# Cross attention's output projection as seven products, with its right operands stored during the first FFN

## The chip, the cores and the metric

The kernel runs on one core of a Trainium2 chip, as one launch. The metric is the device time in microseconds (us), the median of the runs shown. Profiles show one execution, whose span goes from the first to the last instruction.

## The reference

One decoder layer on 1024 tokens of width 1024, in float32, with 256 memory tokens:

```
x <- LN1(alpha*x + 1/2 * SwiGLU_1(x))          D_FF = 2816
x <- LN2(alpha*x + W_out[HGRN2(x) ; SGU(x)])   token mixers
x <- LN3(alpha*x + CrossAttn(x, LN_m(mem)))    4 heads of 256
x <- LN4(alpha*x + 1/2 * SwiGLU_2(x))

def _memory_cross_attention(h, mem, mem_g, mem_b, wq, wk, wv, wo):
    m = _layer_norm(mem, mem_g, mem_b)
    q = (h @ wq).reshape(B, T, X_HEADS, X_HEAD_DIM)
    ...
    p = jax.nn.softmax(s, axis=-1)
    o = jnp.einsum('bhtm,bmhd->bthd', p, v).reshape(B, T, D_MODEL)
    return o @ wo
```

The change concerns the last line, `o @ wo`, a product of 1024 x 1024 by 1024 x 1024, and the sum and norm LN3 behind it.

## The kernel before

Matrix products keep float32 precision by splitting each operand into a high and a low part of type float32r (`split`, `split_w`: ACT copies the high part, DVE subtracts it for the low one). Each product is three matmuls in one bank of PSUM (`mm3`): high by high, high by low, low by high. A matmul takes 128 rows of the contraction and writes 128x512.

The activations stand transposed in SBUF, in two halves of 512 tokens: `xh[half]` and `xl[half]`, eight k-tiles of 128 features each. Weights are read by `load_split`: a load of 512 KB on SP's queue into one of three raw buffers, then the split.

The stages follow each other on TensorE: the start (the memory's norm on GpSimd and ACT, its transposes `ptm`, its keys `psk` and values `psv`, and x transposed, `pt_x`), FFN 1 (up projections `st_gf` and `st_uf` in Strassen's form, then the down projection `dp_f`), the token mixers, their output projection `acc_mx`, cross attention, its output projection `acc_xa`, and FFN 2. FFN 2's first pair of feature tiles (`pg_f`, `pu_f`) is multiplied without Strassen's form, one half of the tokens after the other, so that it can begin while the other half is still normed.

The order of instructions on each engine comes from a scheduler that plays the program through in time. Work that follows a product on other engines is written as a coroutine: `spawn` starts it, it yields the time (in us) of other products that should come first, and `tick(us)` moves all of them on. Waits are taken by each engine in its fixed order.

The output projection runs in three groups of token tiles, (0,1), (2,3,4) and (5,6,7), by `down_group`: for each of eight k-tiles it loads and splits a 128x1024 piece of `xa_w_o`, so it reads the weight three times (`wd_xa`, 24 loads), and multiplies with both column halves. The first group is woven into the attention of the second half of the tokens. Behind a group, `residual_norm` adds the residual on DVE, norms each tile, stores it to `res[2]` and transposes it (`pt_xa`) into `xh` and `xl`, with a copy `xf_xa` for FFN 2's combinations.

Cross attention makes queries `paq`, scores `pss`, probabilities transposed `ptp`, and in `attend` the outputs `pao`, which are split straight from PSUM into `xh` and `xl`.

Before, no DMA is issued by GpSimd; all data transfers go through SP's queue.

Of the kernel before, what the change touches and what calls it, by code (L numbers as in the profile page):

```python
# [15 lines left out]
P = 128  # L16
# [8 lines left out]
H = 4  # L25
# [3 lines left out]
WARM = 32  # L29
LEVELS = [64, 32, 16, 8, 4, 2, 1]  # L30
# [3 lines left out]
def hybrid_layer_kernel(ctx: ExitStack, tc: tile.TileContext, a, out):  # L34
# [29 lines left out]
    # Work that follows a matrix product on other engines runs as a coroutine: where the tensor  # L64
    # engine would wait for it, it yields the time of other products (in us) to issue first.
# [26 lines left out]
    # the tensor engine's clock rises while it works: transposes until the first tile is there  # L92
# [9 lines left out]
    # left and right operands of the products of the FFNs' down projection, by pair of feature tiles  # L102
    lops = dram.tile([7, NF // 2, P, HALF], F32, name="lops")
    rops = dram.tile([2, NF // 2, P, HALF], F32, name="rops")
    res = [dram.tile([T, D], F32, name=f"res{i}") for i in range(3)]

# [5 lines left out]
    def load_raw(view, name, pool=None):  # L112
        if pool is not None:
            raw = pool(f"{name}_r", [P] + list(view.shape[1:]))
            nc.sync.dma_start(raw, view)
            return raw
        raw = wpool.tile([P] + list(view.shape[1:]), F32, tag="raw", bufs=3, name=f"{name}_r")
        nc.sync.dma_start(raw, view)
        return raw
# [10 lines left out]
    def mm3(ps, lh, ll, rh, rl, first, last):  # L130
        nc.tensor.matmul(ps, lh, rh, start=first, stop=False)  # L131
        nc.tensor.matmul(ps, lh, rl, start=False, stop=False)  # L132
        nc.tensor.matmul(ps, ll, rh, start=False, stop=last)  # L133
# [73 lines left out]
    def layer_norm(y, gb, bb, name):  # L207
        """y: [P, 1024] tile, normalized over its free dim in place."""
# [5 lines left out]
    def residual_norm(tt, lag, acc, res_src, gb, bb, dst, name, keep=None):  # L214
        """dst = LN(alpha * res_src + acc) for a token tile, and its transpose."""
# [10 lines left out]
    def down_group(w, nk, grp, operand, res_src, gb, bb, dst, name, keep=None):  # L226
        """dst = LN(alpha * res_src + operand^T @ w) for the token tiles of grp; yields after each k."""
# [20 lines left out]

    def half_sl(hf):
# [28 lines left out]
    def w_combos(w, f1, f2, name, pool=None):  # L278
        """Left operands of the products, in two stages: those of the first part, then all."""
# [48 lines left out]
    def ffn(wg, wu, wd, g, b, res_src, dst, make_xT, xf, name, start=None):  # L328
        """start: products that come before, given what to do late in them; without it, the first pair of
        feature tiles is multiplied without Strassen's form."""  # L330
# [17 lines left out]
        else:  # L348
            f0 = 2
            wts, hts = {}, {}  # L350
            for f, hf in ((0, 0), (1, 0), (0, 1), (1, 1)):
                if (f, hf) == (0, 1):
# [5 lines left out]
                if (f, hf) == (1, 1):  # L358
                    wc[1] = combos(1, f0)
                    ready_u = next(wc[1])  # L360
                if hf == 0:
# [845 lines left out]
```

## Time and profile before

| | |
|---|---|
| time, median of 3 runs | 2039.55 us (2039.29 to 2039.57) |
| span of the profiled execution | 2032.8 us |
| what lies around the span, median less span | 6.75 us |
| TensorE busy | 2015.5 us (99%) |
| DVE, ACT, GpSimd busy | 1504.1, 890.0, 102.5 us |
| first and last product of `acc_mx` | about 1022 and 1152 us |
| output projection `acc_xa` | about 1275 to 1386 us |

How to read it: PE is TensorE's matmul, PEld its weight load, DVE is VectorE, ACT ScalarE, POOL GpSimd, SP the engine that issues DMAs. L131 is line 131 of the kernel, and a line may be that of a helper. A row of a group gives the busy time, the mean length of one in ns, the idle time of the engine just before them and what ended it. Matmuls are pipelined, so the length of one is more than its distance to the next.

### The profile page before, as it was taken

The page shows a single profiled execution, that of the slowest core. Times are in us where ns is not written, and L with a number is a line of the kernel's source. Part 1 is how long each engine was busy: PE and PEld are TensorE (multiplying, and loading weights), DVE is VectorE, ACT ScalarE, POOL GpSimd, SP SyncE. Part 2 cuts the span into 40 slices and gives each one's busy share as a digit, 9 for nine tenths or more (in the row PEclk, how much of TensorE's full clock was granted, in tenths as well). Part 3 has the DMA queues.
Part 4 walks back from the last instruction along what each step waited for, and adds up shares of the span by engine and source line. Part 5 has one row for each costly group of instructions (what it writes and reads, how often), then busy time and mean ns, then how long its engine had stood idle before and what let it go on. Part 6 is the DMA issues. An engine that isn't in the chain of part 4 may idle for free.

```text
span 2032.8 us, 25339 instructions
## 1 busy us (share of the span) xinstructions
PE 2015.5 (99%) x9646; PEld 1689.1 (83%) x9646; DVE 1504.1 (74%) x2246; ACT 890.0 (44%) x1239; POOL 102.5 (5%) x144
## 2 busy tenths in 40 slices
PE   8999999999999999999999999999999999999998
PEld 7888888888888888888888888888888888888886
DVE  5987677677668967948796855678776776776688
ACT  6633333334533467547644344444333333344432
POOL 0000000000002010100110100010000000000021
PEclk8999999999999999999999999999999999999999
DMA  8333233237887632123156522353232332378874
GB/s 263 122 114 119 78 114 119 78 119 250 290 289 261 222 116 73 53 63 105 41 176 228 162 88 74 122 197 119 88 126 82 104 127 81 109 249 291 297 254 172
DMA packets 244250, 306.88 MB, mean 151 GB/s; under 512 B 14368, under 2 KB 154272, under 8 KB 244128
## 3 DMA queue, kind: packets, MB, share of 16 engines
q1 hardware_dynamic: 244128, 305.26, 45.3%
q8 instruction: 76, 1.25, 0.2%
q14 instruction: 46, 0.38, 0.1%
HBM read 234.44 MB, written 70.78 MB: 150 GB/s over the span
## 4 chain that ended last, share of the span: by engine, by line
PE 93%; DVE 3%; DMA 2%; POOL 1%; issue 1%; SPq 0%; ACT 0%; POOLq 0%; DVEq 0%; ACTq 0%
PE st_gf L131 7%; PE st_uf L131 7%; PE st_gf L133 7%; PE st_uf L133 7%; PE st_gf L132 7%; PE st_uf L132 7%; PE dp_f L133 6%; PE dp_f L131 6%; PE dp_f L132 6%; PE psl L939 2%; PE acc_xa L131 1%; PE acc_xa L133 1%; PE acc_xa L132 1%; PE paq L131 1%; PE paq L133 1%; PE paq L132 1%
## 5 line engine op out<-in xcount | busy, mean ns | idle before, releaser
L132 PE MATMUL dp_f<-wd_f_l,ah_f 128*128 128x512 f32 x552 | 213.3, 390 | 0.0
L131 PE MATMUL dp_f<-wd_f_h,ah_f 128*128 128x512 f32 x552 | 208.4, 390 | 0.0
L133 PE MATMUL dp_f<-wd_f_h,al_f 128*128 128x512 f32 x552 | 206.1, 390 | 0.1
L133 PEld LDWEIGHTS dp_f<-wd_f_h,al_f 128*128 128x128 f32 x552 | 103.7, 188 | 22.2 <-DVE al_f L110 0.9
L132 PEld LDWEIGHTS dp_f<-wd_f_l,ah_f 128*128 128x128 f32 x552 | 103.6, 188 | 21.6
L131 PEld LDWEIGHTS dp_f<-wd_f_h,ah_f 128*128 128x128 f32 x552 | 103.6, 188 | 21.2
L109 ACT ACTIVATE wd_f_h<-wd_f_r 128x1024 fp32r<-128x1024 f32 x72 | 73.2, 1022 | 97.7 <-DVE wd_f_r L436 28.3
L110 DVE TENSOR_TENSOR al_f<-ar_f,ah_f 128x1024 fp32r<-128x1024 f32 x72 | 84.5, 1174 | 24.5 <-ACT ah_f L109 23.6
L109 ACT ACTIVATE ah_f<-ar_f 128x1024 fp32r<-128x1024 f32 x72 | 73.3, 1019 | 59.2 <-DMA ar_f<-lops 54.3
L110 DVE TENSOR_TENSOR wd_f_l<-wd_f_r,wd_f_h 128x1024 fp32r<-128x1024 f32 x72 | 84.3, 1175 | 12.5 <-ACT wd_f_h L109 12.2
L316 DVE TENSOR_TENSOR top_uf<-bot_uf,st_uf 128x512 f32<-128x512 f32 x21 | 14.4, 686 | 81.8 <-PE st_uf L133 81.8
L315 ACT ACTIVATE bot_gf<-st_gf 128x512 f32<-128x512 f32 x21 | 12.5, 597 | 137.1 <-PE st_gf L133 137.1
L560 POOL TENSOR_SCALAR nm_f<-nm_f 128x1 f32<-128x1 f32 x8 | 10.7, 1336 | 1198.8 <-ACT xl L559 1198.8
L131 PE MATMUL st_gf<-xh,wg_f_h 128*128 128x512 f32 x168 | 65.4, 389 | 0.0
L133 PE MATMUL st_gf<-xh,wg_f_l 128*128 128x512 f32 x168 | 65.4, 389 | 0.0
L131 PE MATMUL st_uf<-xh,wu_f_h 128*128 128x512 f32 x168 | 65.4, 389 | 0.0
L132 PE MATMUL st_uf<-xl,wu_f_h 128*128 128x512 f32 x168 | 65.4, 389 | 0.0
L133 PE MATMUL st_uf<-xh,wu_f_l 128*128 128x512 f32 x168 | 65.4, 389 | 0.0
L132 PE MATMUL st_gf<-xl,wg_f_h 128*128 128x512 f32 x168 | 65.3, 389 | 0.0
L109 ACT ACTIVATE wg_f_h<-wg_f_r 128x1024 fp32r<-128x1024 f32 x44 | 46.4, 1056 | 36.2 <-PE st_gf L132 29.3
L109 ACT ACTIVATE wu_f_h<-wu_f_r 128x1024 fp32r<-128x1024 f32 x44 | 46.3, 1053 | 35.7 <-issue 27.2
L110 DVE TENSOR_TENSOR wu_f_l<-wu_f_r,wu_f_h 128x1024 fp32r<-128x1024 f32 x44 | 53.6, 1219 | 3.2 <-PE acc_xa L132 3.2
(456 smaller groups left out, 5960.1 us busy)
## 6 DMA issues: line engine op xcount, KB each, us to landing
ar_f<-lops SPq DMA_DIRECT2D x66, 512.0 KB, 5.0
wd_f_r<-in_ffn_w_down_dram SPq DMA_DIRECT2D x56, 512.0 KB, 4.8
wg_f_r<-in_ffn_w_gate_dram SPq DMA_DIRECT2D x44, 512.0 KB, 3.8
wu_f_r<-in_ffn_w_up_dram SPq DMA_DIRECT2D x44, 512.0 KB, 3.8
wd_mx_r<-in_w_out_dram SPq DMA_DIRECT2D x24, 512.0 KB, 3.6
wd_xa_r<-in_xa_w_o_dram SPq DMA_DIRECT2D x24, 512.0 KB, 3.5
lops<-bot_gf SPq DMA_DIRECT2D x21, 512.0 KB, 2.7
lops<-top_uf SPq DMA_DIRECT2D x21, 512.0 KB, 2.8
```

The lines of the kernel that those rows point to most:

```text
L109: order(nc.scalar.activation(hi, src, AF.Copy))
L110: order(nc.vector.tensor_tensor(lo, src, hi.bitcast(F32), op=ALU.subtract))
L131: nc.tensor.matmul(ps, lh, rh, start=first, stop=False)
L132: nc.tensor.matmul(ps, lh, rl, start=False, stop=False)
L133: nc.tensor.matmul(ps, ll, rh, start=False, stop=last)
L315: nc.scalar.activation(b0, product(1), AF.Copy)
L316: nc.vector.tensor_tensor(t0, b0, product(2), op=ALU.add)
L560: nc.gpsimd.tensor_scalar(nmean, nmean, -1.0 / D, None, op0=ALU.mult)
L939: nc.tensor.matmul(psl[:m, (i * NC2 + c) * 64:(i * NC2 + c + 1) * 64] .rearrange("p (n b) -> p n b", b=B), e[:, :m], blk(e, B)[:, :, 1, :] ...
```

## The change

The output projection is written as seven products of half size (the form of Winograd for Strassen's algorithm, which FFN 1 and FFN 2 use already). The blocks are halves of the tokens, of the contraction and of the columns. F is half 0 of the tokens, G half 1.

The right operands, sums and differences of weight blocks, are made and split in the first FFN and lie in DRAM (`sq_ops`) until the attention. `later` is spawned at the end of the start. `prepare_square` lets GpSimd's queue copy blocks of the weight in DRAM and accumulate other blocks onto them; then 14 coroutines `operand` load half a right operand each, let ACT copy the high part and its negative, store both, and accumulate the operand onto the negative, which leaves the low part.

In the attention, `Square.fetch` loads the stored parts straight into the buffers of split weights, and no split is done there. The left operands are combinations of the attended blocks: `attend` copies F's output also to a tile `ao`, which is stored and read again, and makes the differences for G with DVE. The products' results are added onto the residual tiles (`top`, `bot`) one bank at a time. G's tiles are normed with sums taken by ACT, F's with DVE's statistics. FFN 2 begins with half G.

The raw weight buffers are four instead of three (`RAW`). The mixers' output projection stays as it was.

```diff
-        raw = wpool.tile([P] + list(view.shape[1:]), F32, tag="raw", bufs=3, name=f"{name}_r")
+        raw = wpool.tile([P] + list(view.shape[1:]), F32, tag="raw", bufs=RAW, name=f"{name}_r")
...
+    def prepare_square(w, ops, name):
+        wb = w.rearrange("(kb k) (db d) -> kb db k d", kb=2, db=2)
+        sums = {}
+        for p, first, b in ((5, "11", "12"), (7, "22", "12"), (6, 5, "22"), (4, 6, "21")):
+            sums[p] = dram.tile([HALF, HALF], F32, name=f"sum_{name}{p}")
...
+            for rows in halves:
+                nc.gpsimd.dma_start(sums[p][rows], src[rows])
+            yield 6
+            for rows in halves:
+                nc.gpsimd.dma_start(sums[p][rows], add[rows], accum_op=ALU.add)
+            yield 6
...
+        for p in (1, 7, 4, 6, 5, 2, 3):
+            for n in range(2):
+                spawn(operand(sums[p][2 * n * P:2 * (n + 1) * P].rearrange("(i p) d -> p i d", p=P),
+                              ops[p - 1, n], f"{name}_{p}{n}"))
+                yield 13
+
+    def operand(src, dst, name):
+        raw = wpool.tile([P, 2, HALF], F32, tag="raw", bufs=RAW, name=f"pr_{name}")
+        nc.gpsimd.dma_start(raw, src)
+        yield 10
+        hi, neg = (wpool.tile([P, 2, HALF], F32R, tag="whi", bufs=6, name=f"p{i}_{name}") for i in "hn")
+        tc.keep_in_program_order(nc.scalar.activation(hi, raw, AF.Copy))
+        tc.keep_in_program_order(nc.scalar.activation(neg, hi.bitcast(F32), AF.Copy, scale=-1.0))
+        nc.gpsimd.dma_start(dst[0], hi.bitcast(F32))
+        nc.gpsimd.dma_start(dst[1], neg.bitcast(F32))
+        yield 9
+        nc.gpsimd.dma_start(dst[1], src, accum_op=ALU.add)
...
+    class Square:
...
+        def fetch(self, *ps):
+            for p in ps:
+                self.right[p] = []
+                for n in range(2):
+                    hi = wpool.tile([P, 2, HALF], F32R, tag="whi", bufs=6, name=f"sh_{self.name}_{p}{n}")
+                    lo = wpool.tile([P, 2, HALF], F32R, tag="wlo", bufs=5, name=f"sl_{self.name}_{p}{n}")
+                    for i, t in enumerate((hi, lo)):
+                        nc.sync.dma_start(t.bitcast(F32), self.ops[p - 1, n, i])
+                    self.right[p].append((hi, lo))
...
+        def finish(self, x, p2=None):
...
+            self.step(4, x, g, 4, 0)
+            self.step(4, x, g, 4, 1)
...
+            self.tiles(6, y, f, 0, done6, True)
...
+            self.tiles(5, y, g, 0, done5)
...
+                self.tiles(2, z, f, 4, done2, True)
...
+            self.tiles(3, y, f, 0, done3)
+            for e in [e for e in flows if e[0] in self.early]:
+                flows.remove(e)
+                for _ in e[0]:
+                    pass
...
     def start(meanwhile):
         mem_keys(mem_start())
         mem_values(meanwhile)
+        spawn(later())
+
+    def later():
+        yield 20
+        for n, w in (("xa", a["xa_w_o"][0]),):
+            yield from prepare_square(w, sq_ops[n], n)
...
-    first = out_group((0, 1))
+    sq.fetch(1)
+    x = sq.bank("sx")
     for h in range(H):
...
-    run(first)
-    run(out_group((2, 3, 4)))
-    run(out_group((5, 6, 7)))
+    sq.finish(x)
...
-        a["ln4_g"][0], a["ln4_b"][0], res[2], out[0], False, xf2, "f2")
+        a["ln4_g"][0], a["ln4_b"][0], res[2], out[0], False, xf2, "f2", h0=G)
```

Where the instructions come to stand is shown at three places. In the names, `sum_xa` is a sum of weight blocks in DRAM, `pr_xa`, `ph_xa` and `pn_xa` are an operand's raw, high and negated tiles, `sq_xa` the stored operands, `sh_xa`, `sl_xa` fetched parts, `sy_xa`, `sz_xa` banks of the new products. DMASW names the completion of a DMA that GpSimd issued, DMAHW of one that another engine issued.

The first place is GpSimd at the very start of the program, with the memory's norm (`ve_mem` to `nm_mem`). Before:

```order
L89 MEMSET ident 128x128
L97 MEMSET mhalf 128x16
L756 MEMSET ones 128x128
L90 ISA
L90 AFFINE_SELECT ident<-ident 128x128 [waits Pool_49]
L179 TENSOR_SCALAR ve_mem_168<-mv_mem_162 128x1 [waits DVE_49]
L182 TENSOR_TENSOR rs_mem_163<-ve_mem_168,mhalf 128x1 [waits Pool_49]
L651 TENSOR_SCALAR nm_mem_164<-mv_mem_162 128x1
L652 TENSOR_TENSOR nm_mem_164<-nm_mem_164,rs_mem_163 128x1 [waits Pool_49]
```

The same place of GpSimd after:

```order
L90 MEMSET ident 128x128
L98 MEMSET mhalf 128x16
L268 DMA sum_xa_1019<-in_xa_w_o_dram 256x512 x2
L91 ISA
L91 AFFINE_SELECT ident<-ident 128x128 [waits Pool_49]
L268 DMA sum_xa_1108<-in_xa_w_o_dram 256x512 x2
L960 MEMSET ones 128x128
L184 TENSOR_SCALAR ve_mem_172<-mv_mem_166 128x1 [waits DVE_49]
L187 TENSOR_TENSOR rs_mem_167<-ve_mem_172,mhalf 128x1 [waits Pool_49]
L849 TENSOR_SCALAR nm_mem_168<-mv_mem_166 128x1
L271 DMA sum_xa_1019<-in_xa_w_o_dram 256x512 [waits DMASW0_49]
L850 TENSOR_TENSOR nm_mem_168<-nm_mem_168,rs_mem_167 128x1 [waits Pool_49]
```

Four copies of the weight stand ahead of the memory's norm, and the first accumulation, which waits for the first copy, ahead of its last step. The other accumulations and four more copies follow the memory's second tile directly, each with a wait for an earlier one.

The second place is ACT in FFN 1, between the feature tiles 6 and 8 (`bot_uf`, `top_uf` are evacuations of the products' banks, `wg_f` weight splits). Before:

```order
L315 ACTIVATE bot_uf_6_1809<-st_uf_6_1_1810 128x512 [waits DMAHW5_49,PE_49]
L317 ACTIVATE top_uf_6_1808<-st_uf_6_3_1838 128x512 [waits DMAHW6_49,PE_49]
L109 ACTIVATE wg_f_8_4_1936<-wg_f_8_1_r 128x512 [waits DVE_49,Activation_49]
L109 ACTIVATE wg_f_8_a_h<-wg_f_8_sa 128x1024 [waits Activation_49]
L109 ACTIVATE wg_f_8_2_h<-wg_f_8_2_r 128x1024 [waits DMAHW0_49,Activation_49]
L319 ACTIVATE bot_uf_6_1809<-st_uf_6_5_1854 128x512 [waits PE_49]
```

ACT at that place after:

```order
L513 ACTIVATE bot_uf_6_1870<-st_uf_6_1_1871 128x512 [waits DMAHW3_49,PE_49]
L286 ACTIVATE ph_xa_1899<-pr_xa_1812 128x1024 [waits DMASW3_49,DMASW0_49]
L287 ACTIVATE pn_xa_1900<-ph_xa_1899 128x1024 [waits Activation_49]
L515 ACTIVATE top_uf_6_1869<-st_uf_6_3_1906 128x512 [waits DMAHW5_49,PE_49]
L517 ACTIVATE bot_uf_6_1870<-st_uf_6_5_1924 128x512 [waits PE_49]
L286 ACTIVATE ph_xa_1983<-pr_xa_1919 128x1024 [waits DMASW7_49]
L287 ACTIVATE pn_xa_1984<-ph_xa_1983 128x1024 [waits Activation_49]
L113 ACTIVATE wg_f_8_1_h<-wg_f_8_1_r 128x1024 [waits DMAHW7_49,DMASW2_49]
L113 ACTIVATE wg_f_8_4_2013<-wg_f_8_1_r 128x512 [waits DMASW4_49,DVE_49]
```

The copies of the operands wait for loads that GpSimd issued, ahead of evacuations, and FFN 1's own weight splits wait for stores of operands.

The third place is TensorE where the projection ends and FFN 2 begins (half G is `xh_116`, half F `xh_115`). Before:

```order
L131 MATMUL acc_xa_1_11048<-wd_xa_7_h,xh_116 128x512
L132 MATMUL acc_xa_1_11048<-wd_xa_7_l,xh_116 128x512
L133 MATMUL acc_xa_1_11048<-wd_xa_7_h,xl_118 128x512
L131 MATMUL pg_f_0_0_11366<-xh_115,wg_f_0_h 128x512 [waits DVE_49]
L132 MATMUL pg_f_0_0_11366<-xl_117,wg_f_0_h 128x512
```

TensorE at that place after:

```order
L163 MATMUL pt_xa_0_11315<-ident,r_xa 128x128 [waits PE_49,Activation_49]
L163 MATMUL pt_xa_0_11315<-ident,r_xa 128x128 x3
L163 MATMUL pt_xa_4_11351<-ident,r_xa 128x128 [waits PE_49,Activation_49]
L163 MATMUL pt_xa_4_11351<-ident,r_xa 128x128 x3
L138 MATMUL sy_xa_10968<-sh_xa_11031,xl_117 128x512
...
L138 MATMUL sy_xa_10968<-sh_xa_11035,xl_117 128x512
L136 MATMUL pg_f_0_1_11445<-xh_116,wg_f_0_h 128x512 [waits DVE_49,Activation_49]
L136 MATMUL pu_f_0_1_11498<-xh_116,wu_f_0_h 128x512 [waits DVE_49]
```

Before, FFN 2 began with half F, whose tiles had been transposed while the projection's last group ran. After, it begins with half G, and the transposes of its last tile stand seven matmuls ahead; five of the seven are left out here.

More of the change, by code (lines that the diff above doesn't have):

```diff
@@ L29 @@
 WARM = 32
+RAW = 4
 LEVELS = [64, 32, 16, 8, 4, 2, 1]
@@ L128, in load_split, with mm3 @@
         return split_w(load_raw(view, name), name)
[L130 to L133, printed above, removed]
+    def mm3(ps, lh, ll, rh, rl, first, last, more=False):
+        nc.tensor.matmul(ps, lh, rh, start=first, stop=False, skip_group_check=more)
+        nc.tensor.matmul(ps, lh, rl, start=False, stop=False, skip_group_check=more)
+        nc.tensor.matmul(ps, ll, rh, start=False, stop=last, skip_group_check=more)
     def wcol(w, c):
@@ L1124, in attend @@
         pTh, pTl = pts[half, h]
+        n = h % 2
+        if half == F:
+            ao = gt(f"ao{h}", (P, 2, HALF))
+        elif h < 2:
+            sq.s[n] = gt(f"s3_xa{n}", (P, 2, HALF))
         for j in range(2):
@@ L1130, in attend, with attended_again @@
                 mm3(ps, vmh[m][:, cs], vml[m][:, cs], pTh[:, m, :], pTl[:, m, :], m == 0, m == 1)
-            split(ps, xh[half][:, c, :], xl[half][:, c, :])
+            if half == F:
+                nc.scalar.activation(ao[:, j, :], ps, AF.Copy)
+                split(ps, xh[half][:, c, :], xl[half][:, c, :])
+            elif h < 2:
+                nc.vector.tensor_tensor(sq.s[n][:, j, :], sq.a1[0][n][:, j, :], ps, op=ALU.subtract)
+            else:
+                split(ps, xh[half][:, c, :], xl[half][:, c, :])
+                nc.vector.tensor_tensor(sq.s[n][:, j, :], sq.s[n][:, j, :], ps, op=ALU.add)
+        if half == F:
+            nc.sync.dma_start(ao_dram[h], ao)
+        elif h < 2:
+            sq.put(sq.s[n], G, 0, n)
+    def attended_again(h):
+        t = gt(f"ao_again{h}", (P, 2, HALF))
+        nc.sync.dma_start(t, ao_dram[h])
+        return t
+    sq = Square(sq_ops["xa"], res[1], (None, None), res[2], "xa", F,
+                [{}, lambda n: attended_again(2 + n)], xf2)
     kTh, kTl = ([gt(f"kT{t}{j}", (P, 4, MEM), F32R) for j in range(2)] for t in "hl")
```

165 lines of the change are left out of this document (142 added, 23 removed).

## Prediction

> **What bounds the kernel now.** I read the page first, then the TensorE waits, then the timeline and the windows of the stages that the change touches. The page's span, its busy line and the shares of its chain:
>
> ```profile
> span 2032.8 us, 25339 instructions
> ...
> PE 2015.5 (99%) x9646; PEld 1689.1 (83%) x9646; DVE 1504.1 (74%) x2246; ACT 890.0 (44%) x1239; POOL 102.5 (5%) x144
> ...
> PE 93%; DVE 3%; DMA 2%; POOL 1%; issue 1%; SPq 0%; ACT 0%; POOLq 0%; DVEq 0%; ACTq 0%
> ```
>
> TensorE is busy for 99% of the span and is 93% of the chain. All its waits, by whom it waited for (us in total, times, longest):
>
> ```profile
> PE ptm L660 <- ACT mem L653: 3.3, 2, 2.2
> PE warm L95 <- POOL ident L90: 1.6, 1, 1.6
> PE psk L131 <- ACT mTh L109: 1.1, 1, 1.1
> PE ptm L660 <- DVE mf L663: 0.9, 1, 0.9
> PE psk L132 <- DVE mTl L110: 0.5, 1, 0.5
> PE psl L939 <- DVE r_mx L220: 0.4, 1, 0.4
> PE psk L131 <- ACT wk_h L109: 0.4, 1, 0.4
> PE pt_x L158 <- ACT xf_x L172: 0.3, 1, 0.3
> ```
>
> These are 8.5 us, and all but the 0.4 of psl lie in the start, in the memory's norm and keys. After it TensorE never waits for the attention's output projection, for FFN 1 or for FFN 2. So a matrix product that goes saves its whole price, while work taken from DVE or ACT saves nothing, and the change can lose time only where it makes TensorE wait anew. A busy time over start-to-start distance misleads here, since products overlap; the timeline of the projection (start, us, operation) has the price:
>
> ```profile
> 1375.78 0.39 PE L132 MATMUL acc_xa<-wd_xa_l,xh 128*128 128x512 f32 x1
> ...
> 1383.96 0.39 PE L132 MATMUL acc_xa<-wd_xa_l,xh 128*128 128x512 f32 x1
> ```
>
> With both ends 37 products are in these rows: 36 distances in 8.18 us, 0.227 us each. The shown length of 0.39 us is no price. The windows (us, busy of PE, PEld, DVE, ACT, POOL, granted clock, DMA share, GB/s) of FFN 1 agree, with 280 us for 1237 instructions, 0.226:
>
> ```profile
> 160.00:440.00 280.00, 280.00 (x1237) 231.86 (x1236) 200.73 (x262) 92.43 (x116) 0.00 (x0) 1.00 0.32 103
> 480.00:560.00 80.00, 80.00 (x354) 66.24 (x354) 56.26 (x60) 39.07 (x42) 0.00 (x0) 1.00 0.84 288
> 1300.00:1400.00 100.00, 100.00 (x481) 83.46 (x480) 76.45 (x111) 39.82 (x79) 13.62 (x16) 1.00 0.53 182
> ```
>
> **The change part by part.** *The products.* The projection before, and the splits of its weight:
>
> ```profile
> L131 PE MATMUL acc_xa<-wd_xa_h,xh 128*128 128x512 f32 x128 | 50.2, 395 | 0.0
> ...
> L110 DVE TENSOR_TENSOR wd_xa_l<-wd_xa_r,wd_xa_h 128x1024 fp32r<-128x1024 f32 x24 | 29.3, 1222 | 25.5 <-PE paq L133 16.9 <-PE acc_xa L132 7.8 <-issue 0.3
> L109 ACT ACTIVATE wd_xa_h<-wd_xa_r 128x1024 fp32r<-128x1024 f32 x24 | 25.5, 1063 | 56.0 <-PE paq L132 24.5 <-PE acc_xa L133 24.3 <-DVE st_xa L192 3.0
> ```
>
> There are three such rows, 3 x 128 = 384 products. Seven products of half size in each of three dimensions have 7 x 48 = 336 of the same 128x512 form. 48 fewer at 0.227 us are **-10.9 us**, all on the path. (By the 395 ns it would be 19 us; that counts the overlap twice.) The transposes stay.
>
> *DVE and ACT in the attention.* The nearest rows for the new combinations and copies:
>
> ```profile
> L220 DVE SCALAR_TENSOR_TENSOR r_xa<-r_xa,acc_xa 128x512 f32<-128x512 f32 x16 | 10.4, 678 | 0.0
> L315 ACT ACTIVATE bot_gf<-st_gf 128x512 f32<-128x512 f32 x21 | 12.5, 597 | 137.1 <-PE st_gf L133 137.1
> ```
>
> DVE loses 24 x 1.22 = 29.3 us and gains some 24 operations of 128x512 at 0.68 and 10 of 128x1024 at 1.22, 28.5 us; less the statistics of four tiles, which ACT takes. ACT loses 25.5 and gains 12 copies at 0.60, 6 and 8 passes of 128x1024 at 1.06: 22 us. In 1300 to 1400 DVE is busy 76% and ACT 40% without one TensorE wait, and both fall a little: **0**, covered by that idle time. The 28 fetches and eight transfers of the attended half replace 24 loads: some 36 x 0.5 MB where there were 12 MB; the stage's DMA share of 0.53 has room, with 0.84 and 288 GB/s borne without a wait in FFN 1's down projection. If this cover went, a product would wait for its fetched operand.
>
> *The start.* The four copies of weight blocks are issued by GpSimd at about 1 us, not behind the start, and the memory's norm has an accumulating transfer ahead of its last step. The start before, in the timeline, the chain and the windows:
>
> ```profile
> 7.46 0.19 POOL L652 TENSOR_TENSOR nm_mem<-nm_mem,rs_mem 128x1 f32<-128x1 f32 x1
> 7.69 1.24 ACT L653 ACTIVATE mem<-mem,nm_mem,rs_mem 128x1024 f32<-128x1024 f32 x1 [0.48 <-POOL nm_mem L652]
> ...
> 9.03 9.36 DMA wk_r<-in_xa_w_k_dram
> 18.41 1.07 ACT wk_h L109
> ...
> 20.37 7.24 DMA wk_r<-in_xa_w_k_dram
> ...
> 0.00:5.00 5.00, 3.44 (x18) 3.44 (x19) 0.43 (x1) 0.00 (x0) 0.87 (x8) 1.00 0.59 196
> 5.00:10.00 5.00, 2.17 (x18) 1.70 (x16) 2.49 (x6) 3.30 (x3) 2.45 (x8) 1.00 0.89 226
> 10.00:15.00 5.00, 2.56 (x12) 1.86 (x12) 3.27 (x4) 2.99 (x4) 0.00 (x0) 0.64 1.08 380
> 15.00:20.00 5.00, 4.46 (x21) 4.26 (x21) 3.60 (x8) 2.21 (x3) 0.00 (x0) 0.50 1.07 366
> 20.00:25.00 5.00, 5.00 (x37) 5.00 (x36) 2.92 (x5) 0.63 (x1) 0.00 (x0) 0.83 1.12 317
> ```
>
> From 10 to 25 us the DMA engines are full, and the chain runs through the loads of the key weight: what is added ahead of them delays TensorE. Four copies of 0.52 MB at 380 GB/s are 5.5 us of full engines. Free before 10 us are 0.41 x 5 + 0.11 x 5 = 2.6. So **+2.9 us**. Below: 0, if the engines' shown share leaves more room than it says; no gain, since nothing is taken out of the start. Above: the accumulating transfers (eight, with four more copies) follow each as soon as its copy has landed; if four of them, another 2.1 MB, also run before 25 us, it is 11 - 2.6 = 8.4, and with GpSimd's step held behind a landing of some 2 us, 10. I take 2.9, because the accumulating ones are issued one behind the other, each waiting for a landing, so they spread out, and behind 30 us the engines have room.
>
> *FFN 1.* 14 operands, paced 13 us apart by the flow, add 56 transfers of 0.5 MB and 28 ACT passes at 1.06, 30 us. DMA: 29 MB in 14 x 13 = 182 us are 161 GB/s on top of 103: 264, under the 288 that the down projection bore. ACT goes from 33% busy to about 50%. But an ACT copy waits, in ACT's fixed order, for a GpSimd-issued load, and FFN 1's own weight splits wait for the stores that free their buffers; behind them stand the evacuations of TensorE's banks. So what counts is whether GpSimd's chain keeps the pace. The rows nearest to its links:
>
> ```profile
> wg_f_r<-in_ffn_w_gate_dram SPq DMA_DIRECT2D x44, 512.0 KB, 3.8
> ...
> lops<-bot_gf SPq DMA_DIRECT2D x21, 512.0 KB, 2.7
> ...
> 6.30 0.43 SPq L118 DMA_DIRECT2D wk_r<-in_xa_w_k_dram  x1
> ...
> L560 POOL TENSOR_SCALAR nm_f<-nm_f 128x1 f32<-128x1 f32 x8 | 10.7, 1336 | 1198.8 <-ACT xl L559 1198.8
> ...
> L560 POOL TENSOR_SCALAR nm_f<-nm_f x8: 207/1003/3140, 640.4 to 1978.6; 128x1 f32<-128x1 f32 x8
> ```
>
> Per operand GpSimd issues a store (behind ACT's first copy), the next load, a second store (behind the second copy), and an accumulation behind the landing of that store, 2.7 us. With two copies the cycle is 2.1 + 2.7 + 4d = 4.8 + 4d, d being GpSimd's time for one issue, which no row of before has: it issues no transfer. From below d is SP's 0.43, cycle 6.5; from above the 3.14 us that a GpSimd instruction of one column took at the longest beside a busy DVE, cycle 17.4. I take the median of that row, 1.0, since DVE is as busy in FFN 1 (72%) as there: cycle 8.8, under 13, and **0 us** lost, hidden behind TensorE's own products. At 17.4 it would be 14 x 4.4 = 62 us. The turning point is d = 2.05.
>
> The Trainium skill ("SBUF — State Buffer", its note on the "DVE blocks DMA" trap and the section Who interferes with whom) says that descriptors of a GpSimd-issued DMA are written by GpSimd and are held up while DVE runs a two-port operation, 3.1 us against 0.62 in its example, but that tensor_tensor has no such mode. By its 3.1 us the cycle would be 17.2 and the sum 59 us higher; by its list of operations FFN 1, whose DVE work is almost all tensor_tensor and scalar_tensor_tensor, would be spared. No run here shows which.
>
> *Into FFN 2.* Its first products take the half whose norms come early, since the other ends last. But the transposes of that half's last tile stand only seven projection products, 7 x 0.227 = 1.6 us, ahead of FFN 2's first. What follows a tile's transposes, on 1/4 of a tile each:
>
> ```profile
> L110 DVE TENSOR_TENSOR xl<-xf_xa,xh 128x256 fp32r<-128x256 f32 x32 | 12.1, 420 | 6.9 <-ACT xh L109 6.9
> L109 ACT ACTIVATE xh<-xf_xa 128x256 fp32r<-128x256 f32 x32 | 11.8, 424 | 0.0
> L172 ACT ACTIVATE xf_xa<-pt_xa 128x256 f32<-128x256 f32 x32 | 10.7, 383 | 14.7 <-PE pt_xa L158 14.7
> ```
>
> ACT does the last tile's four copies, 4 x 0.38, then in the new order a weight split of 1.06, then the high parts at 0.42. FFN 2's first product needs the first high part alone: 1.5 + 1.1 + 0.4 = 3.0 us, of which 1.6 are covered: 1.4. Were all four and the last low part needed, it would be 4.7 - 1.6 = 3.1. I take **+2.0 us**, nearer to the first, since each k-tile feeds 12 products before the next is read. Below 0, if the seven products are themselves late and cover more; above 5, when two more weight splits of 1.06 get ahead.
>
> **The sum**: -10.9 + 2.9 + 0 + 2.0 = -6.0 us. The profiled span goes from 2032.8 to about 2026.8; the median is 2039.55, 6.75 us above the span, and I let that part stand: 2033.6.
>
> **The rivals.** *A, the start eats the gain.* The full engines of 10 to 25 us speak for it, against it that each accumulation waits for a landing. With +8.4 there, -10.9 + 8.4 + 2.0 = -0.5: 2039. *B, slower: GpSimd's chain paces FFN 1.* Place: ACT's queue, where a copy that waits for its load holds the evacuations. For it speaks nm_f's longest of 3.14 us, against it its shortest of 0.21. At d halfway between mean and longest, 2.24 us, the cycle is 13.8, 0.8 too long, 14 x 0.8 = 11 us: 2045. With every issue held as long as nm_f's longest, 3.14 us, it is the 62 us above, 2096; of B's chance I give that 0.07, since one row in eight shows it. B decides from d = 2.23, where the loss passes the 10.1 us that lie between the forecast and the upper bound of no change. *C, all is hidden*: with nothing lost in the start or into FFN 2 the whole 10.9 stay: 2028.7. The idle 41% of the first 5 us speak for it, the full 15 behind them against it; I count it with the forecast's side.
>
> **How the numbers follow.** A measurement of this kernel can tell about 0.2%, 4.1 us, from no change, so faster means below 2035.5 and slower above 2043.6. The forecast's side, from C's 2028.7 up to 2035.5 (start under 4.9, chain within its pace): 0.42. A, between the bounds: 0.30. B, with the start's and the handover's upper ends together (-10.9 + 10 + 5 = +4.1): 0.28. The likeliest case's own range is 2029 to 2036. The one for 8 in 10 begins at C's 2029 and reaches to 2050, d = 2.34 with the forecast's other terms (14 x 1.16 = 16.2 us); a longer chain is left out, the 0.07 of the longest one in it.
>
> **What would show it.** In the changed profile: 336 projection products 0.227 us apart; the waits of TensorE for the memory's norm and the key weight up by some 3 us and no more; no TensorE wait for bot_gf, top_gf or their weights between 160 and 440; one wait of about 2 us at the first gate product of FFN 2, for the high part of the transposed tile. Wrong it would be by a GpSimd issue of over 2 us in FFN 1, by the accumulations running in the first 25 us, or by a fetched operand that lands late, a wait at the products of the projection.

## The result, and the profile after

The changed kernel takes 2058.9 us (median of three, 2058.12 to 2065.69), the one before 2039.55 in the same runs: ratio 1.0102, 95% interval 1.0076 to 1.0128, slower by about 1%. Forecast was 2033.6, with 2050 as the upper end. In the later runs the kernel before had medians of 2035.5 to 2036.6 (13 to 17 runs each); against those the change costs 22 to 23 us. The profiled execution of the changed kernel is the longest of its three, 2065.69 us with a span of 2064.0: only 1.7 us lie around a span, so the 6.75 that the prediction carried over was a difference between two executions.

The page of the changed kernel: TensorE's busy time is as before although it runs 48 matmuls fewer (its mean granted clock is 0.992, before 0.996), but its share of the chain fell from 93% to 78%, DMA's rose from 2% to 7%:

```profile
span 2064.0 us, 25469 instructions
PE 2016.7 (98%) x9598; PEld 1683.9 (82%) x9598; DVE 1497.0 (73%) x2242; ACT 910.2 (44%) x1275; POOL 158.8 (8%) x220
PE 78%; DMA 7%; DVE 6%; issue 4%; POOL 2%; SPq 1%; ACT 1%; DVEq 0%; POOLq 0%; ACTq 0%
```

TensorE's waits, the eight largest, where before there were eight in all with 8.5 us:

```profile
PE ptm L858 <- ACT mem L851: 6.8, 2, 5.9
PE pg_f L137 <- DVE xl L114: 3.8, 1, 3.8
PE dp_f L136 <- ACT ah_f L113: 3.8, 3, 2.3
PE dp_f L136 <- ACT wd_f_h L113: 3.5, 2, 2.6
PE warm L96 <- POOL ident L91: 3.3, 1, 3.3
PE psk L136 <- ACT wk_h L113: 3.3, 2, 2.1
PE dp_f L136 <- DVE db_f L781: 2.7, 2, 1.5
PE psv L137 <- DVE wv_l L114: 2.3, 1, 2.3
```

They lie in four places: the start (ptm, warm, psk, psv), FFN 1's up projections (2.5 us of waits for wu_f), both down projections (dp_f), and FFN 2's first pair (pg_f). dp_f is the surprise: the change moves nothing there. Where the time went is seen best by stage. The table has, for every kernel of this study, the length of a stage less its length before, in us, from the starts of the first matmuls in the profiled executions (start: to the first st_gf; up: to the first dp_f; middle: FFN 1's down projection, mixers and attention, to the last pao; projection: to the first pg_f; first pair: to FFN 2's first st_gf; down 2: from FFN 2's first dp_f to the end; what lies between is unchanged everywhere). The last columns are the timed medians, of the kernel and of the one before in the same call.

| kernel | start | up | middle | projection | first pair | down 2 | median | before |
|---|---|---|---|---|---|---|---|---|
| after | 10.1 | 8.2 | 10.1 | -10.8 | 7.7 | 6.0 | 2058.9 | 2039.6 |
| raw4_before | -2.9 | 4.5 | 6.2 | 0.0 | 0.0 | 9.4 | 2048.9 | 2035.5 |
| raw3_after | 20.3 | 22.3 | 3.2 | -11.7 | 6.7 | 1.9 | 2079.6 | 2035.5 |
| prep_only | 19.6 | 27.1 | 3.8 | 0.0 | 0.0 | 1.8 | 2086.1 | 2035.5 |
| square_only | -0.9 | 0.5 | 0.7 | -11.7 | 8.0 | -0.2 | 2035.9 | 2035.5 |
| hand_early | -0.1 | 0.6 | 0.7 | -13.0 | 4.7 | 4.5 | 2031.3 | 2036.2 |
| held | -2.8 | 5.5 | 6.5 | -10.8 | 8.1 | 5.9 | 2049.6 | 2036.2 |
| own_raw | 27.6 | 3.1 | 2.6 | -11.7 | 7.2 | 2.6 | 2068.4 | 2036.2 |
| all_three | -0.3 | 1.1 | 3.3 | -12.9 | 4.7 | 1.7 | 2029.4 | 2036.2 |
| held_norm | 9.3 | 3.6 | 5.2 | -10.8 | 7.1 | 7.8 | 2056.9 | 2036.6 |
| prep_late_own | 0.0 | 0.4 | 1.9 | 0.0 | 0.0 | 0.6 | 2037.7 | 2036.6 |

A row is one execution, so its sum is not the difference of the medians: for the changed kernel, whose profiled execution is its longest, it is 31.2 us against 22 to 23. Start and up belong together, because in every kernel the last of the memory's value products (psv) come behind the first st_gf. The number behind "to" is the start of the last one, before and then in the changed kernel:

```profile
L133 PE MATMUL psv<-wv_h,mTl x32: 389/389/477, 47.7 to 73.2; 128*128 128x512 f32 x32
```

```profile
L138 PE MATMUL psv<-wv_h,mTl x32: 389/389/628, 60.0 to 92.2; 128*128 128x512 f32 x32
```

The last of them is 19.0 us later, and start and up together are 18.3 us longer. From there to the first dp_f are 416.6 us with 1826 products, where before 417.4 us had 1843; at the 0.226 us of a product that is a loss of some 3 us. So most of the 8.2 us under up is the start's, and about 3 are FFN 1's own, as many as in raw4_before, which prepares nothing (417.2 us with 1827).

The seven products do what they should: the projection is 10.8 us shorter. In its groups each of the three lines has 48 matmuls into sx, 48 into sy and 16 into sz, 336 in all, and none of them waited:

```profile
L136 PE MATMUL sx_xa<-sh_xa,xh 128*128 128x512 f32 x48 | 18.9, 394 | 0.0
L136 PE MATMUL sy_xa<-sh_xa,xh 128*128 128x512 f32 x48 | 18.9, 394 | 0.0
```

Everything else is given away around them. Four causes were in question: the fourth raw buffer, the preparation in the start, the preparation in FFN 1, and the handover to FFN 2.

### The profile page after: what moved, and what is told of

Read it like the earlier page. It is cut to its first block, busy times and chain, and to the rows that moved or that the text cites. A ratio compares the mean times of both kernels' runs of the same rounds, so it can differ in the third digit from the quotient of the medians.

```text
span 2064.0 us, 25469 instructions
## 1 busy us (share of the span) xinstructions
PE 2016.7 (98%) x9598; PEld 1683.9 (82%) x9598; DVE 1497.0 (73%) x2242; ACT 910.2 (44%) x1275; POOL 158.8 (8%) x220
## 4 chain that ended last, share of the span: by engine, by line
PE 78%; DMA 7%; DVE 6%; issue 4%; POOL 2%; SPq 1%; ACT 1%; DVEq 0%; POOLq 0%; ACTq 0%
PE st_uf L138 6%; PE st_uf L136 6%; PE st_uf L137 6%; PE st_gf L138 6%; PE st_gf L136 6%; PE st_gf L137 6%; PE dp_f L138 3%; PE dp_f L137 3%; PE dp_f L136 3%; DMA wd_f_t<-rops 2%; PE psl L1143 2%; DMA ar_f<-lops 1%; PE acc_mx L137 1%; PE acc_mx L136 1%; PE acc_mx L138 1%
## 5 line engine op out<-in xcount | busy, mean ns | idle before, releaser
L136 PE MATMUL dp_f<-wd_f_h,ah_f 128*128 128x512 f32 x552 | 214.6, 391 | 7.7 <-ACT ah_f L113 3.8
L113 ACT ACTIVATE ah_f<-ar_f 128x1024 fp32r<-128x1024 f32 x72 | 73.2, 1019 | 120.2 <-DMA ar_f<-lops 117.2
L758 POOL TENSOR_SCALAR nm_f<-nm_f 128x1 f32<-128x1 f32 x8 | 4.5, 558 | 888.5 <-ACT xl L757 888.5
L514 DVE TENSOR_TENSOR top_uf<-bot_uf,st_uf 128x512 f32<-128x512 f32 x21 | 14.4, 688 | 71.2 <-PE st_uf L138 61.8
L113 ACT ACTIVATE wg_f_h<-wg_f_r 128x1024 fp32r<-128x1024 f32 x44 | 46.4, 1054 | 33.7 <-PE st_gf L137 20.3
L114 DVE TENSOR_TENSOR wg_f_l<-wg_f_r,wg_f_h 128x1024 fp32r<-128x1024 f32 x44 | 53.6, 1219 | 5.0 <-ACT wg_f_h L113 5.0
```

Source lines behind the costliest of these rows:

```text
L113: order(nc.scalar.activation(hi, src, AF.Copy))
L114: order(nc.vector.tensor_tensor(lo, src, hi.bitcast(F32), op=ALU.subtract))
L136: nc.tensor.matmul(ps, lh, rh, start=first, stop=False, skip_group_check=more)
L514: nc.vector.tensor_tensor(t0, b0, product(2), op=ALU.add)
L758: nc.gpsimd.tensor_scalar(nmean, nmean, -1.0 / D, None, op0=ALU.mult)
```

## Experiments

**The fourth buffer alone (raw4_before).**

```diff
-        raw = wpool.tile([P] + list(view.shape[1:]), F32, tag="raw", bufs=3, name=f"{name}_r")
+        raw = wpool.tile([P] + list(view.shape[1:]), F32, tag="raw", bufs=4, name=f"{name}_r")
```

> The kernel before with four raw weight buffers instead of three, nothing else. In the profile after, 16 of the 31 us by which the span is longer lie in the two down projections (10.1 from the first to the last dp_f of FFN 1, 6.0 in FFN 2), where the change touches nothing but this number; loads of weights then stand ahead of the loads of left operands on SP's queue. Theory R (the fourth buffer costs it): 2045 to 2056, with TensorE waits for ah_f in both down projections. Rival P (the preparation, or chance from run to run, delays them): 2036 to 2042, no such waits.

Measured: 2048.9 us against 2035.5, ratio 1.0063 (1.0046 to 1.0079). Theory R holds: one more buffer, and nothing else, costs the kernel before 13 us, in the two down projections (6.2 and 9.4 in its row) and, some 3 us, in FFN 1's up projections, of which an earlier start takes a part back (start and up together are 1.6). In the down projections TensorE waits for ah_f, which it never did before:

```profile
PE dp_f L131 <- ACT ah_f L109: 2.7, 4, 0.9
```

ACT's wait for the left operands, in the kernel before and then in this one (us, times, longest):

```profile
ACT ah_f L109 <- DMA ar_f<-lops: 54.3, 34, 3.9
```

```profile
ACT ah_f L109 <- DMA ar_f<-lops: 119.4, 37, 17.5
```

Twice the wait, and its longest from 3.9 to 17.5 us. In SP's order, of the 72 loads of left operands 66 have one to three more weight loads ahead of them than before: a weight load may go one buffer earlier, so it goes ahead of a load that is needed sooner. In a stage whose DMA share is 0.84 that is a place in a queue which counts; a load ar_f takes a median of 5.9 us to land, before 5.0:

```profile
ar_f<-lops SPq DMA_DIRECT2D x66, 512.0 KB, 5.9
```

That is the row of raw4_before; the changed kernel has the same 5.9. ACT's wait goes with the number of buffers in the other runs too: 117.2 us in the changed kernel and 117.5 in held, with four, 58.3 in raw3_after and 60.7 in all_three, with three for the weights.

**The change with three buffers (raw3_after).**

```diff
-RAW = 4
+RAW = 3
```

> The changed kernel with three raw buffers as before. Theory R: the waits of the down projections go, about 10 to 16 us less than after's 2058.9: 2043 to 2049. Rival P: 2055 to 2062. Both: the start still 10 us later, since the preparation stands as it was.

Measured: 2079.6 us, ratio to before 1.0223 (1.0203 to 1.0243). Both theories missed. The down projections did recover (middle 10.1 to 3.2, down 2 6.0 to 1.9), as R has it, but the start and FFN 1 lost 24 us more, and here FFN 1 loses much: the last psv is 25.1 us later than before, but start and up together are 42.6 us longer. The operands' raw tiles share the three buffers with FFN 1's weights (own_raw, below, takes that alone away). So the fourth buffer has a use in the change: with it the operands starve FFN 1 less. Where no operands are prepared, it costs more than it gives.

**The preparation alone (prep_only).** The kernel before, three buffers, with `prepare_square` and `operand` added and their results unused.

> The kernel before, three raw buffers, with the preparation of the operands in the start and FFN 1 as in the change, and the old projection; the prepared operands are not used. Theory S (the preparation costs what the stages show: 10.1 us in the start and 8.2 in FFN 1's up projections): 2054 to 2060. Rival H (these delays came from the changed order with four buffers, GpSimd's transfers are hidden): under 2046. If the down projections are delayed here too, with three buffers, that speaks for P.

Measured: 2086.1 us, ratio 1.0244 (1.0227 to 1.026): more than theory S, and far from H. SP's loads of weights waited 26.4 us for ACT's copy out of an operand's raw tile, whose buffer they need; and TensorE's largest wait is one of FFN 1, for a weight that landed late:

```profile
SPq L120 <- ACT ph_xa L280: 26.4, 6, 13.8
```

```profile
PE st_uf L135 <- DVE wu_f_l L112: 10.8, 1, 10.8
```

That weight's load was issued at 346.0, just behind such a copy (344.7 to 345.8), and took 12.8 us to land, where the median of these loads is 3.9.

The down projections are nearly undisturbed here (3.8 and 1.8), with three buffers and the whole preparation: rival P, that the preparation delays them, falls as the main cause. A rest stays unexplained: the middle is 1.9 to 3.8 us longer in all runs with the preparation and three buffers for the weights, and 0.7 in the two without it.

**The seven products alone (square_only).** Three buffers; no preparation; one high and one low tile are stored behind FFN 1, and every fetch reads these, so the traffic is that of the change and the projection's values are not.

```diff
-                        nc.sync.dma_start(t.bitcast(F32), self.ops[p - 1, n, i])
+                        nc.sync.dma_start(t.bitcast(F32), one_op[i])
...
-        spawn(later())
```

> The changed kernel, three raw buffers, without the preparation: one high and one low tile of the weight are split and stored once behind FFN 1, and all 28 fetches read these two, so the traffic and the work in the attention are those of the change and the values are not. Theory W (the seven products give 10.7 us up to FFN 2, and the handover to FFN 2 takes 7.7 back): 2035 to 2038. Rival C (fetches hidden, handover caused by something else): 2027 to 2031, without a TensorE wait for xl at FFN 2's first products.

Measured: 2035.9 us against 2035.5, ratio 0.9994 (0.9981 to 1.0007): no difference. Theory W holds by stage: 11.7 us gained in the projection, 8.0 lost in FFN 2's first pair, at one wait:

```profile
PE pg_f L138 <- DVE xl L115: 4.2, 1, 4.2
```

In the changed kernel that place reads as follows in the timeline (start, us, engine, operation; rows are left out at the dots). DVE works through half F's norms and a weight split, and only then through the four low parts of half G's last tile, for which TensorE waits:

```profile
1404.42 1.28 DVE L207 SCALAR_TENSOR_TENSOR r_xa<-r_xa,mv_xa,g_xa 128x1024 f32<-128x1024 f32 x1
...
1405.62 1.28 DVE L197 BATCH_NORM_STATS2 st_xa<-r_xa 128x6 f32<-128x512 f32 x2
...
1407.40 1.22 DVE L114 TENSOR_TENSOR wg_f_l<-wg_f_r,wg_f_h 128x1024 fp32r<-128x1024 f32 x1
1408.54 1.43 DVE L114 TENSOR_TENSOR xl<-xf_xa,xh 128x256 fp32r<-128x256 f32 x4
...
1409.01 0.79 PE L137 MATMUL pg_f<-xl,wg_f_h 128*128 128x512 f32 x1 [3.80 <-DVE xl L114]
...
1410.03 0.63 PE L136 MATMUL pg_f<-xh,wg_f_h 128*128 128x512 f32 x1
1410.46 0.63 PE L137 MATMUL pg_f<-xl,wg_f_h 128*128 128x512 f32 x1
```

The high parts had been there by 1405. The wait is 3.8 us, but behind it the products stand 0.43 us apart instead of 0.227. The windows (us, busy of PE, PEld, DVE, ACT, POOL, granted clock, DMA share, GB/s) show why: the granted clock falls to a half.

```profile
1404.00:1408.00 4.00, 1.20 (x4) 0.67 (x4) 4.00 (x6) 0.89 (x3) 0.00 (x0) 1.00 0.86 249
1408.00:1412.00 4.00, 2.99 (x7) 2.41 (x8) 3.96 (x8) 0.00 (x0) 0.63 (x1) 0.51 0.05 16
1412.00:1416.00 4.00, 4.00 (x13) 3.10 (x13) 3.96 (x6) 0.00 (x0) 2.06 (x3) 0.63 0.36 146
1416.00:1420.00 4.00, 4.00 (x23) 3.41 (x22) 3.74 (x8) 2.24 (x8) 1.41 (x3) 1.00 0.39 158
```

From 1409 to about 1415 that is some 6 us at half speed, 3 us more. The Trainium skill ("TensorE: Matmul & The Clock Gate", Part 1) has the array at half its clock after an idle window of about 3.4 us and back after as long a busy one, with 427 ns between 512-column products while cold; the 0.43 agrees, the 6 us are longer than one such window. By length alone the half clock can't be told here: in prep_only it followed a wait of 2.0 us (for db_f, at 659), shorter than the window that the Trainium skill states, while the changed kernel's 2.6 us for wd_f_h left the clock at 1.00. The windows behind that wait of prep_only, with the clock at 0.54 and 0.61:

```profile
660.00:662.00 2.00, 2.00 (x6) 1.54 (x5) 2.00 (x4) 0.25 (x1) 0.00 (x0) 0.54 1.03 377
662.00:664.00 2.00, 2.00 (x7) 1.56 (x6) 2.00 (x5) 1.06 (x1) 0.00 (x0) 0.61 0.58 215
```

**The handover mended (hand_early).** square_only, with the last transposes of half G flushed behind the first tile of product 3, which TensorE then takes in program order.

```diff
             def done3(t):
+                if t == 0:
+                    flush()
...
-            self.tiles(3, y, f, 0, done3)
+            with tc.manual_schedule(engines={mybir.EngineType.PE}):
+                self.tiles(3, y, f, 0, done3)
```

> Square alone (no preparation, its fetches reading one stored pair of tiles), with the last transposes of half G moved ahead of most of product 3 on TensorE, so that DVE's low parts of that tile stand ahead of half F's norms. Theory D (the 4.2 us wait for xl, and the half clock behind it, come from DVE's order: the low parts stood behind half F's work): the 8.0 us between the first gate product and FFN 2's first Strassen product go, 2035.9 less 7 to 8: 2028 to 2029. Rival W (the weight splits of FFN 2's first pair are late themselves): 2033 to 2037, with a wait at the same products for wg_f or wu_f.

Measured: 2031.3 us against 2036.2, ratio 0.9969 (0.9956 to 0.9982), 4.6 us under square_only. The wait for xl is gone, and what is left there is a short one for the high part, after which the clock stays at 1.00:

```profile
PE pg_f L137 <- ACT xh L114: 0.9, 1, 0.9
```

Theory D holds in kind, with a bit more than half of its 8 us. Twelve products of product 3 now stand behind FFN 2's first ones (2.7 us that the table moves from one column to the next), so projection and first pair together gain 8.3 instead of square_only's 3.7. Down 2 was 4.5 us longer in this profiled execution, with a wait for a bank's evacuation; all_three has the same edit and 1.7 there, so I do not put it down to the edit, and it stays unexplained.

**The preparation behind the start (held).** In DRAM each first copy's place is written before by a tiny transfer from the last transposed tile of x.

```diff
             for rows in halves:
+                if first not in sums:
+                    nc.gpsimd.dma_start(sums[p][rows][0:1, 0:P], xl[1].bitcast(F32)[0:1, KT - 1, 3 * P:4 * P])
                 nc.gpsimd.dma_start(sums[p][rows], src[rows])
```

> The changed kernel, where GpSimd's first copies of weight blocks wait for the last transposed tile of x (a small transfer from it is written ahead of them to the same place), so that nothing of the preparation runs in the start. Theory S (the start lost its 10 us to GpSimd's own queue and to full DMA engines): about 10 us less than 2058.9: 2047 to 2051, FFN 1's first st_gf back at 62 to 63 us. Rival M (the accumulations cost as much wherever they run, since GpSimd's chain then paces FFN 1): 2055 to 2065.

Measured: 2049.6 us, ratio to before 1.0063 (1.0041 to 1.0084), 9.3 us under the change. Theory S: the start's loss goes, and FFN 1 does not take it over. Start and up together are 2.7 us longer than before, of which raw4_before has 1.6 without any preparation.

**Queue or engines (held_norm).** As held, but the tiny transfer comes from the memory's second normed tile, so it goes at 10.9 us, when GpSimd has done the norm, and the copies follow at 16.1. Against held:

```diff
-xl[1].bitcast(F32)[0:1, KT - 1, 3 * P:4 * P]
+mT["ms"][0:1, 0:P]
```

> The changed kernel, where GpSimd's first copies wait for the memory's second normed tile (about 10 us) instead of the program's begin: GpSimd's queue is then free for the memory's norm, but the copies and accumulations still run beside the start's loads. Held behind the start altogether, it was 2049.6; at the program's begin, 2058.9. Theory Q (the queue: the norm stood behind GpSimd's own issues): 2048 to 2052, first st_gf at 60 to 64 us. Rival E (the DMA engines: the loads of the key and value weights come late): 2054 to 2062, first st_gf at 68 to 74 us, and TensorE waits for wk and wv but not for mem.

Measured: 2056.9 us, ratio 1.0092 (1.007 to 1.0114). Rival E: the memory's norm is in time (first psk at 14.0 us, before 14.4), but the start still ends 9.3 us late, because the key weight comes late. The wait, and the window in which TensorE is busy for 6.14 of 10 us with the DMA engines full:

```profile
PE psk L136 <- ACT wk_h L113: 4.5, 2, 3.4
...
30.00:40.00 10.00, 6.14 (x33) 5.64 (x33) 1.41 (x2) 2.75 (x8) 0.92 (x1) 0.69 1.01 225
```

In the changed kernel itself both happen. GpSimd's fourth copy was issued only at 10.6 us, after 6.9 us in which nothing shown held it, and the norm's last steps stood behind it; the whole set of sixteen transfers kept the engines full:

```profile
10.63 0.57 POOL L268 DMA_DIRECT2D sum_xa<-in_xa_w_o_dram  x1 [6.88 <-issue]
...
14.19 1.24 ACT L851 ACTIVATE mem<-mem,nm_mem,rs_mem 128x1024 f32<-128x1024 f32 x1 [7.13 <-POOL nm_mem L850]
...
10.00:15.00 5.00, 0.00 (x0) 0.00 (x0) 0.00 (x0) 0.81 (x1) 3.76 (x9) 0.71 1.05 311
15.00:20.00 5.00, 3.10 (x13) 2.33 (x13) 2.01 (x3) 3.25 (x4) 0.57 (x3) 0.50 1.04 305
20.00:25.00 5.00, 2.95 (x15) 2.65 (x13) 4.89 (x9) 2.10 (x3) 0.74 (x1) 0.50 1.07 325
```

That fits a delay of the queue which is hidden under the later one of the engines. It is not shown apart: held_norm is 2 us below the changed kernel, within the spread of their runs, and its copies start 15 us later.

**A buffer of their own (own_raw).** The change with three buffers for the weights and one, under another tag, for the operands.

```diff
-RAW = 4
+RAW = 3
...
-        raw = wpool.tile([P, 2, HALF], F32, tag="raw", bufs=RAW, name=f"pr_{name}")
+        raw = wpool.tile([P, 2, HALF], F32, tag="praw", bufs=1, name=f"pr_{name}")
```

> The changed kernel with three raw buffers for the weights again, and a buffer of its own, one, for the operands' raw tiles. Theory B (with four shared buffers the loads of the down projections run too far ahead, with three shared the operands starve FFN 1; an own buffer avoids both): the 16 us of the down projections go, 2041 to 2047. Rival Q (it is the pace of the operands that starves FFN 1, whoever owns the buffer): 2060 to 2085, with waits for wu_f as with three shared ones.

Measured: 2068.4 us against 2036.2, ratio 1.0151 (1.013 to 1.0172), slower than the change. By its total it speaks for Q, by its stages for B: up falls from 8.2 to 3.1, the middle from 10.1 to 2.6, down 2 from 6.0 to 2.6. The run that differs from it by the operands' buffer alone is raw3_after: 11 us slower, with 22.3 under up, so sharing the three buffers costs FFN 1 some 20 us there; SP's wait for ph_xa, 25.9 us in raw3_after, is gone. What rose against the change is the start, by 17.5 us. The first operand's load now had a free buffer at once and joined the copies (issued at 10.8 us), and two accumulations came to stand between the steps of the memory's norm on GpSimd; the second, in the timeline, was issued only at 27 us:

```profile
PE ptm L858 <- ACT mem L851: 20.4, 2, 11.2
...
27.25 1.02 POOL L271 DMA_DIRECT2D sum_xa<-in_xa_w_o_dram  x1 [7.82 <-issue]
27.96 0.54 POOL L850 TENSOR_TENSOR nm_mem<-nm_mem,rs_mem 128x1 f32<-128x1 f32 x1
```

The expectation had left that out. Here GpSimd's queue costs more than the engines: TensorE's waits for the memory's norm are 20.4 us, those for the key and value weights 6.5.

**The preparation, late and with its own buffer (prep_late_own).** prep_only with the edits of held and own_raw, and the first operand's load held in the same way.

> The kernel before with the preparation alone, held behind the start and with an operand buffer of its own, beside three for the weights; the prepared operands are not used. Prepared in the start and with the three buffers shared, it took 2086. Theory N (the transfers and ACT passes themselves are hidden in FFN 1, as the prediction had it; what they cost before was the start and the buffer): 2035 to 2039. Rival F (56 transfers of 0.5 MB in FFN 1 cost something of their own): 2042 to 2060, with TensorE waits between 100 and 340 us.

Measured: 2037.7 us against 2036.6, ratio 1.0005 (0.9994 to 1.0016), where prep_only had 1.0244. Theory N: 72 transfers and 28 ACT passes in FFN 1 are hidden; up is 0.4 us longer. The 50 us of prep_only were almost all the start and the shared buffers, which the two edits take away together.

**All three (all_three).** held, own_raw (with the first operand's load held too) and hand_early in the changed kernel.

> The changed kernel with all three: preparation held behind the start (its first load too), own raw buffer, early transposes of half G. If the parts add up (10 + 16 + 8 us off 2058.9, and what FFN 1's up projections lose stays): 2022 to 2030, faster than before by 6 to 14 us. If the preparation moves its cost into FFN 1: 2034 to 2045.

Measured: 2029.4 us against 2036.2, ratio 0.9965 (0.9953 to 0.9978): faster than the kernel before by 7 us and, across calls, than the changed one by 29, at the slow end of what the parts promised. Its three largest waits:

```profile
PE dp_f L136 <- DVE db_f L790: 3.7, 2, 2.6
PE ptm L867 <- ACT mem L860: 3.1, 2, 2.0
PE warm L96 <- POOL ident L91: 1.6, 1, 1.6
```

Of the 10.9 us of 48 products some 7 arrive.

## Why the prediction was wrong, point by point

The products' gain came as forecast. What failed is the rest of the sum: it had no term for the fourth raw buffer (13.4 us), and the terms for the start (2.9, measured 9.3) and for the handover (2.0, measured 7.7) were too small.

- **The products, -10.9.** Right: -10.8 in the changed kernel, -11.7 alone.
- **The fourth buffer.** The step that failed most, by not being there: the prediction's parts have no term for it. I took a larger number of buffers for room that costs nothing. Alone it is +13.4 us (2048.9 against 2035.5). In the diff it was one constant; in SP's order it moved weight loads ahead of ar_f in both down projections, stages that the profile showed at a DMA share of 0.84.
- **The start, +2.9.** Right in place, too small: about +9.3 (2058.9 against held's 2049.6), near the upper end of 10. In the profiled execution, 6.8 us longer than the median, it is more: start and up together are 15.6 us above held's. I had the eight accumulations spread out into engines that have room behind 30 us. They did spread, issued from 12.9 to 83.8 us, but the room was not there: from 10 to 80 us the DMA share lies between 0.95 and 1.14, where before it was 0.55 to 0.86 from 30 to 45. Nor did the engines move 380 GB/s, as I had counted, but 305 to 325 from 10 to 25 us. The wait behind GpSimd's queue, which I kept for the upper end, came true as well; held_norm suggests that it was covered.
- **FFN 1, 0, and rival B.** The term was right for the transfers themselves (prep_late_own: up +0.4). GpSimd's issue, which I took as 1.0 us, measured 0.6 to 1.1 in the mean:

```profile
L291 POOL DMA_DIRECT2D sq_xa<-sum_xa x8 | 8.8, 1099 | 49.0 <-DMA sq_xa<-pn_xa 49.0
L289 POOL DMA_DIRECT2D sq_xa<-pn_xa x14 | 8.3, 594 | 40.5 <-issue 24.9 <-ACT wu_f L113 5.1 <-ACT pn_xa L287 4.8
```

  The landing that I took as 2.7 us, from a store of SP's, was off by more: 6.1 in the median for the store ahead of the accumulation. With it the cycle is about 2.1 + 6.1 + 3.4 = 11.6, still under 13; measured are 13.9 us from one operand's last accumulation to the next (176.8 to 357.3 for 14), and 13.4 in prep_late_own. No issue itself took 3 us behind DVE, as the Trainium skill's note in "SBUF — State Buffer" (the "DVE blocks DMA" trap) would have it for two-port operations; FFN 1's DVE operations, tensor_tensor and scalar_tensor_tensor, are not in its list of those, and the trace agrees. But five of the 14 second stores came only after 2.2 to 7.9 us in which nothing shown held GpSimd (the 24.9 us of issue above): my sign for B, an issue of over 2 us, was there in that form, without a cost that prep_late_own shows. What I missed is the third resource beside queue and engines, the raw buffer: shared with the weights it costs FFN 1 some 20 us with three buffers (raw3_after against own_raw). With four, as in the change, held shows about 1 us more than raw4_before in start and up together.
- **The handover, +2.0.** Measured +7.7. I followed the high parts through ACT's order, for which the wait was 1.0 us, and left DVE's order out, where the four low parts stood behind norms of the other half; and I priced a wait at its length, when the half clock behind it added 3 us.
- **The attention, 0.** Right: no wait of more than 0.4 us in it, and every fetched operand in time.
- **The chances.** Rival B carried the slower side with the wrong mechanism. A had the start's size nearly right, 8.4 against 9.3, but with the handover at 2.0 and no buffer term it came to 2039. The largest term was in no case.

The parts add up: 13.4 (buffer, raw4_before) + 0.4 (products with handover, square_only) + 1.0 (late preparation, prep_late_own), each measured alone, and 9.3 (start, the change less held) give 24.1 against the 22 to 23 that the change costs. They are no price list for other orders: the buffer taken out of the change alone made it 21 us slower. What stays open: whether in the down projections it is the place in SP's queue or the sharing of the full engines that makes ar_f late; both follow from the same order, and no run took them apart. Nor was the cause tried of GpSimd's 6.9 us before its fourth copy.

## What to carry to other kernels

A buffer count is a change of order: where loads of different urgency share a queue, one more buffer lets the less urgent ones go first, so look at what moves in the stages that the change doesn't name. Work that has no dependency starts at the program's begin however late it is written; tie it by data to the point where it may start, and give it buffers of its own. Look at the granted clock behind a wait of TensorE, since the wait can cost more than its length, and follow each operand that a product needs through every engine's order, not the first one alone.

## What the runs showed of the hardware

In the changed kernel GpSimd-issued transfers of 512 KB landed in 6.1 to 10.9 us in the median, by kind, most SP-issued ones of the same size behind the start in 3 to 6. Whether that is the queue is not shown: the transfers differ in kind, and they ran at other times. Three of the rows:

```profile
sq_xa<-pn_xa POOLq DMA_DIRECT2D x14, 512.0 KB, 6.1
sum_xa<-in_xa_w_o_dram POOLq DMA_DIRECT2D x12, 512.0 KB, 9.0
sh_xa<-sq_xa SPq DMA_DIRECT2D x14, 512.0 KB, 4.3
```

A wait of 3.8 us of TensorE was followed by 6 us at half the granted clock, while the wait of 0.9 us that hand_early has in its place left it at 1.00. Between them both occur: half clock behind 2.0 us in prep_only, none behind 2.6 us in the changed kernel.
